# A rotary-embedding kernel on one core: a read of one row of `x` put first on ScalarE's DMA ring

## The chip, the cores and the metric

The kernel runs on one core of one Trainium2 chip. A time is the device time of one execution in microseconds (us). The core has five engines with instruction queues of their own: TensorE (PE) for matrix products, VectorE (DVE), ScalarE (ACT) and GpSimd (POOL) for elementwise work, and SyncE (SP), which here only issues DMA transfers. Transfers between the memory (HBM) and the core's SBUF are issued by SyncE and by ScalarE, each on a ring of its own, and are carried out by 16 DMA engines that both rings share.

## What is computed

Rotary position embedding with cached tables. `x` has the shape (8, 8, 1024, 64), the tables (1024, 32), all in float32:

```python
half = x.shape[-1] // 2
x_first, x_second = x[..., :half], x[..., half:]
out_first = x_first * cos_cached - x_second * sin_cached
out_second = x_first * sin_cached + x_second * cos_cached
return np.concatenate([out_first, out_second], axis=-1)
```

## The kernel before

`x` and the output are taken as 8 blocks (u = 0 to 7) of 128 partitions by 64 rows of 64 numbers; a block has 2 MB, and a partition holds 64 rows in sequence. All of `x` stays in SBUF, in the tiles `w0` to `w3`, which also have room for products (`sv`). The result is written over `x` in place and stored from there.

**Loads.** Line 76 has SyncE load the sine table, line 77 has ScalarE load the cosine table, each as 32 partitions by 1024 numbers (128 KB), into a part of `w0` that is free at that time (`rs`, `rc`). Then SyncE issues all loads of `x`: block 0 in two halves (line 81), blocks 1 to 7 whole (line 83). SyncE has nothing else to do but the stores (line 142), which come later in its queue.

**Tables.** A partition needs 64 rows of both tables, even partitions other ones than odd. GpSimd builds a unit matrix `plus` (lines 86, 87); ScalarE, whose first compute instruction brings a load of its function table with it, copies from it the selection matrix `sel` (line 89) and the negative `minus` (line 91). TensorE multiplies `sel` with the loaded tables and so spreads the first 32 rows of the sine table (`en`) and of the cosine table (`ec`) over 128 partitions (line 156), first `en`, then `ec`. For the other 32 rows VectorE shuffles the sine table and then the cosine table over 32 partitions (line 159), and ScalarE (line 160) and GpSimd (line 162) copy these to the other partitions. The shuffle of the cosine table and the product with it are the first readers of `rc`.

**Work.** Block 0 comes first: VectorE multiplies its first half with the tables straight from `en` and `ec` (line 106, called from 163 to 166), ScalarE copies its second half into PSUM (line 113, tile `pre`), VectorE multiplies that (line 172), and GpSimd adds up the products (lines 109, 110). Blocks 1 to 7 are cut into chunks of 24, 24 and 16 rows. For each, ScalarE copies the chunk into PSUM (`st`), VectorE makes both products in one instruction, and the sums are made either by GpSimd or, for 16 rows at a time, by TensorE (lines 184, 185) with ScalarE copying the result back (line 190). Half of block 2 is done by GpSimd alone. The order of all this is written out by hand in the lists `on_pe`, `back` and `behind`; a block is stored when its sums are done, the last block in three pieces.

The schedule is manual: each engine runs its instructions in the order in which the function issues them, and waits are set where an instruction reads or writes what another one wrote or read. The lines of the change stand between the definition of `rs` and `rc` and the two loads of the tables.

Of the kernel before, what the change touches and what calls it, by code (L numbers as in the profile page):

```python
# [8 lines left out]
def kernel(  # L9
# [7 lines left out]
    nc = tc.nc  # L17
    fp32 = mybir.dt.float32
# [3 lines left out]
    b, h, seq, hd = x.shape  # L22
# [12 lines left out]
    xf = x.rearrange("b h s d -> (b h s d)").rearrange(  # L35
        "(u p m) -> u p m", p=P, m=F)
# [4 lines left out]
    const = ctx.enter_context(tc.tile_pool(name="const", bufs=1))  # L41
# [31 lines left out]


    rs, rc = sv[3][0:Q, 0:C], sv[3][0:Q, C:2 * C]
    nc.sync.dma_start(out=rs, in_=sin_cached.rearrange("(q n) j -> q (n j)", q=Q))
    nc.scalar.dma_start(out=rc, in_=cos_cached.rearrange("(q n) j -> q (n j)", q=Q))

# [3 lines left out]
    for u in range(1, n_u):  # L82
# [7 lines left out]
                   in_=plus[0:Q, 0:Q:2].unsqueeze(1).to_broadcast([Q, 2 * P // Q, Q // 2]))  # L90
# [172 lines left out]
```

## Time and profile before

| | us |
|---|---|
| median of 7 runs | 85.33 |
| lowest, highest | 85.25, 85.5 |
| the profiled execution | 85.22 |
| its span, first to last instruction | 83.4 |

The profile is of one execution. A line of its group view gives the kernel's line, the engine, the operation, the tiles written and read, and how often, how long and after what idle time it ran; "q" behind an engine's name (SPq, ACTq) means its instruction queue, which issues DMAs. Busy time over the span: VectorE 82%, GpSimd 80%, TensorE 52%, ScalarE 49%.

| transfers, from the page | |
|---|---|
| moved | 33.82 MB in 2832 packets, 405 GB/s over the span |
| read, written | 17.04 MB, 16.78 MB |
| SyncE's queue | 2784 packets, 96.1% of 16 engines' span |
| ScalarE's queue | 48 packets, 0.4% |
| sine table, issue to landing | 3.0 us |
| cosine table, issue to landing | 3.4 us |

"Landing" is the time at which the transfer's semaphore tells that all of it has arrived. The DMA share of a stretch is the mean busy share of the 16 DMA engines in it.

### The profile page before, as it was taken

Reading aid. Unit: us, or ns where it says so; the run is one execution under the profiler, and the core shown is the slowest. Engines: PE = TensorE matmul, PEld = TensorE weight load, DVE = VectorE, ACT = ScalarE, POOL = GpSimd, SP = SyncE. Lnnn points to the kernel's source line nnn. Section 1 sums busy time; section 2 is a strip of 40 time slices with the busy share of each in tenths; the row PEclk is TensorE's granted clock in tenths of the full one; section 3 lists DMA queues with packets and bytes.
Section 4 is the critical chain, followed back from the end, with each engine's and each line's share of the span. In section 5 each row is a group of like instructions: output and inputs, shape, how many; then the busy total and the mean of one; then the engine's idle time right before and its main releaser. Section 6 shows DMA issues by size and latency. Waiting matters only on the chain.

```text
span 83.4 us, 386 instructions
## 1 busy us (share of the span) xinstructions
PE 43.7 (52%) x80; PEld 16.7 (20%) x80; DVE 68.5 (82%) x30; ACT 40.7 (49%) x36; POOL 67.1 (80%) x36
## 2 busy tenths in 40 slices
PE   0199920004991694949869494971964991000000
PEld 0133200002430332405133240411412330000000
DVE  0193999999999999999999999999999995890000
ACT  4409695364068548196176856675359208100000
POOL 3009809999999999999999999999999999991000
PEclk9999999999999999999999999999998579985555
DMA  2999999899998999999999999999999999999991
GB/s 31 295 428 448 432 424 456 377 487 393 424 456 377 487 393 440 440 401 479 377 393 456 409 448 432 432 432 416 456 401 440 440 432 440 416 440 383 424 416 65
DMA packets 2832, 33.82 MB, mean 405 GB/s; under 512 B 336, under 2 KB 336, under 8 KB 784
## 3 DMA queue, kind: packets, MB, share of 16 engines
q1 hardware_dynamic: 2784, 33.69, 96.1%
q10 hardware_dynamic: 48, 0.13, 0.4%
HBM read 17.04 MB, written 16.78 MB: 405 GB/s over the span
## 4 chain that ended last, share of the span: by engine, by line
POOL 64%; issue 13%; PE 5%; DMA 4%; DVE 3%; POOLq 2%
POOL w L110 26%; POOL w L109 24%; POOL w L106 14%; PE en L156 5%; DMA w<-in_sin_cached_dram 4%; DVE w L106 3%; POOLq L258 2%; POOLq L109 0%; POOLq L106 0%
## 5 line engine op out<-in xcount | busy, mean ns | idle before, releaser
L106 DVE TENSOR_TENSOR w<-st,tb 128x3072 f32<-128x3072 f32 (+2 forms) x19 | 54.7, 2952 | 1.2 <-ACT st L113 1.2
L113 ACT COPY st<-w 128x1536 f32<-128x1536 f32 (+1 forms) x19 | 24.9, 1310 | 15.7 <-DVE w L106 14.7
L184 PE MATMUL acc<-w,plus 128*128 128x512 f32 x36 | 21.1, 670 | 21.6 <-ACT w L190 12.6
L109 POOL TENSOR_TENSOR w<-w 128x1024 f32<-128x1024 f32 (+3 forms) x11 | 23.8, 2163 | 0.2
L110 POOL TENSOR_TENSOR w<-w 128x1024 f32<-128x1024 f32 (+3 forms) x11 | 23.8, 2164 | 0.0
L184 PEld LDWEIGHTS acc<-w,plus 128*128 128x128 f32 x36 | 6.7, 208 | 35.0 <-ACT w L190 19.2
L190 ACT COPY w<-acc 128x1024 f32<-128x1024 f32 x9 | 9.1, 1009 | 9.4 <-PE acc L185 9.4
L106 POOL TENSOR_TENSOR w<-w,tb 128x1280 f32<-128x1280 f32 x4 | 11.6, 2908 | 0.2
L185 PE MATMUL acc<-w,minus 128*128 128x512 f32 x18 | 10.8, 686 | 0.0
L185 PE MATMUL acc<-w,plus 128*128 128x512 f32 x18 | 9.2, 592 | 0.0
L162 POOL COPY tb<-tb 32x2048 f32<-32x2048 f32 x2 | 3.8, 1886 | 5.1 <-DVE tb L159 5.1
L156 PE MATMUL en<-w,sel 32*128 32x512 f32 x4 | 3.7, 1088 | 3.9 <-DMA w<-in_sin_cached_dram 3.9
L185 PEld LDWEIGHTS acc<-w,minus 128*128 128x128 f32 x18 | 4.0, 223 | 5.2 <-issue 5.2
L106 DVE TENSOR_TENSOR w<-pre,tb 128x4096 f32<-128x4096 f32 x1 | 4.4, 4415 | 0.0
L185 PEld LDWEIGHTS acc<-w,plus 128*128 128x128 f32 x18 | 3.4, 190 | 4.5 <-issue 4.5
L109 POOL TENSOR_TENSOR w<-w,w 128x1024 f32<-128x1024 f32 x1 | 2.3, 2326 | 2.2 <-issue 2.2
L156 PE MATMUL ec<-w,sel 32*128 32x512 f32 x4 | 3.6, 1056 | 0.0
L160 ACT COPY tb<-tb 32x2048 f32<-32x2048 f32 x1 | 1.9, 1897 | 3.3 <-DVE tb L159 3.3
L106 DVE TENSOR_TENSOR w<-w,en 128x2048 f32<-128x2048 f32 x1 | 2.3, 2287 | 1.4 <-PE en L156 1.4
L159 DVE LOAD_MASK_SELECT tb<-w x2 | 0.0, 8 | 3.8 <-DMA w<-in_sin_cached_dram 3.8
L159 DVE STREAM_SHUFFLE tb<-w 32x1024 f32<-32x1024 f32 x2 | 2.5, 1279 | 0.0
L106 DVE TENSOR_TENSOR w<-w,ec 128x1024 f32<-128x1024 f32 x2 | 2.4, 1217 | 0.0
(18 smaller groups left out, 14.2 us busy)
## 6 DMA issues: line engine op xcount, KB each, us to landing
w<-in_x_dram SPq DMA_DIRECT2D x7, 2048.0 KB, 24.8
out_dram<-w SPq DMA_DIRECT2D x7, 2048.0 KB, 10.5
w<-in_x_dram SPq DMA_DIRECT2D x2, 1024.0 KB, 6.3
out_dram<-w SPq DMA_DIRECT2D x2, 768.0 KB, 6.6
out_dram<-w SPq DMA_DIRECT2D x1, 512.0 KB, 6.6
w<-in_cos_cached_dram ACTq DMA_DIRECT2D x1, 128.0 KB, 3.4
w<-in_sin_cached_dram SPq DMA_DIRECT2D x1, 128.0 KB, 3.0
```

Source lines behind the costliest of these rows:

```text
L106: eng.tensor_tensor(out=o, in0=a, in1=t, op=TT.mult)
L109: eng.tensor_tensor(out=o[:, :, 0], in0=c[:, :, 0], in1=s[:, :, 1], op=TT.subtract)
L110: eng.tensor_tensor(out=o[:, :, 1], in0=c[:, :, 1], in1=s[:, :, 0], op=TT.add)
L113: nc.scalar.copy(out=pt[:, :(n1 - n0) * hd], in_=xt[u][:, n0 * hd:n1 * hd])
L156: nc.tensor.matmul(part, sel, r, start=True, stop=True)
L159: nc.vector.stream_shuffle(t[0:Q, H:], flat(r), odd)
L160: nc.scalar.copy(out=tb4[Q:2 * Q, H:], in_=tb4[0:Q, H:])
L162: nc.gpsimd.tensor_copy(out=tb4[k * Q:(k + 1) * Q, H:], in_=tb4[0:Q, H:])
L184: nc.tensor.matmul(a[:, k], plus, xr[:, :, k], start=True, stop=False)
L185: nc.tensor.matmul(a[:, k], plus if k else minus, sr[:, :, 1 - k], start=False, stop=True)
L190: nc.scalar.copy(out=rows(xt[u], n0, n0 + G), in_=a)
L258: with _tile.TileContext(nc) as tc:
```

## The change

A tile `row` of one partition by 64 numbers is added to the pool `const`, and ScalarE's first DMA becomes a read of the first row of block 0 of `x` into it. The cosine table is the second DMA on that ring. Nothing reads `row`; SyncE's transfers and all compute are as before.

```diff
     rs, rc = sv[3][0:Q, 0:C], sv[3][0:Q, C:2 * C]
+
+    row = const.tile([1, hd], fp32, name="row")
+    nc.scalar.dma_start(out=row, in_=xf[0][0:1, 0:hd])
     nc.sync.dma_start(out=rs, in_=sin_cached.rearrange("(q n) j -> q (n j)", q=Q))
     nc.scalar.dma_start(out=rc, in_=cos_cached.rearrange("(q n) j -> q (n j)", q=Q))
```

## The prediction

> **What bounds the kernel now.** I read the page's busy shares and its DMA line first, then a table of stretches with the DMA share of each, then the list of instructions in the first 14 us, then SyncE's waits.
>
> The DMA rows of the page, in 40 slices of 2.09 us:
>
> ```profile
> DMA  2999999899998999999999999999999999999991
> GB/s 31 295 428 448 432 424 456 377 487 393 424 456 377 487 393 440 440 401 479 377 393 456 409 448 432 432 432 416 456 401 440 440 432 440 416 440 383 424 416 65
> ```
>
> No compute engine fills its row like this: VectorE is busy 82% of the span and GpSimd 80%. The transfers work from the second slice to the last but one. The table of stretches (length, then each engine's busy time, TensorE's clock, DMA share, GB/s) makes it sharper:
>
> ```profile
> 1.50:2.00 0.50, 0.00 (x0) 0.00 (x0) 0.00 (x0) 0.50 (x1) 0.00 (x0) 1.00 1.04 115
> 2.00:2.50 0.50, 0.00 (x0) 0.00 (x0) 0.00 (x0) 0.49 (x2) 0.00 (x0) 1.00 0.37 106
> 2.50:3.00 0.50, 0.00 (x0) 0.00 (x0) 0.00 (x0) 0.48 (x2) 0.00 (x0) 1.00 1.37 426
> 3.00:4.00 1.00, 0.13 (x1) 0.16 (x1) 0.23 (x2) 0.00 (x0) 0.00 (x0) 1.00 0.93 291
> 4.00:20.00 16.00, 7.04 (x9) 2.37 (x9) 14.59 (x9) 8.77 (x8) 11.35 (x6) 1.00 1.03 435
> ...
> 70.00:80.00 10.00, 0.00 (x0) 0.00 (x0) 3.70 (x5) 1.15 (x2) 5.38 (x4) 0.72 0.98 417
> 80.00:81.00 1.00, 0.00 (x0) 0.00 (x0) 0.00 (x0) 0.00 (x0) 0.00 (x0) 0.50 1.02 418
> ```
>
> From 4 us to 81 us the engines' share is 1.0 (a packet is counted where it starts, hence 1.37 beside 0.37). So the end is the start of the stream, plus 33.8 MB at 417 to 435 GB/s, plus the last landing. The chain of waits on the page runs through GpSimd, but GpSimd ends at 75.4 us, and for 6 us after it only transfers work. A compute step that ends earlier gains nothing. One that ends later costs only where the stream would run dry.
>
> How near is that? SyncE issues stores 0 to 6 at 21.65, 35.27, 47.77, 52.39, 57.01, 63.78 and 70.31 us, and three pieces of the last block at 71.91, 75.41 and 75.84. When store 6 is issued, 17.04 MB of reads and six stores of 2.10 MB had been handed out, 29.62 MB; summing GB/s times length over all stretches up to 70.31 us gives 29.09 MB moved. The 0.53 MB left last 1.27 us at 417 GB/s. A new transfer needs about 1.02 us from its issue to its first packet (the sine table: issued at 0.74, first packet at 1.76 in the packet records). So compute may slip about **0.25 us** before the stream has a hole; store 6 has the least cover (store 5, by the same sum, has 3 us).
>
> The start, from the list of instructions (start, duration, instruction, what ended the idle time before):
>
> ```profile
> 0.73 0.41 ACTq L77 DMA_DIRECT2D w<-in_cos_cached_dram  x1
> ...
> 0.74 0.39 SPq L76 DMA_DIRECT2D w<-in_sin_cached_dram  x1
> ...
> 1.18 1.28 ACT L89 ACT_TABLE_LOAD   x1 [1.18 <-PEq L247]
> 1.18 0.89 SPq L81 DMA_DIRECT2D w<-in_x_dram  x2
> ...
> 3.87 3.75 PE L156 MATMUL en<-w,sel 32*128 32x512 f32 x4 [3.87 <-DMA w<-in_sin_cached_dram]
> ...
> 4.96 1.28 DVE L159 STREAM_SHUFFLE tb<-w 32x1024 f32<-32x1024 f32 x1
> ...
> 7.65 2.29 DVE L106 TENSOR_TENSOR w<-w,en 128x2048 f32<-128x2048 f32 x1 [1.41 <-PE en L156]
> ```
>
> The compute chain starts from the sine table: landed at 3.74 (3.0 after its issue), four matmuls, then VectorE at 7.65, after which VectorE hardly idles until 72 us. The cosine table lands at 0.73 + 3.4 = 4.13 and is first read at 4.96.
>
> **The change, part by part.** It adds one DMA of 256 bytes on ScalarE's ring, ahead of the cosine table, and 256 bytes of SBUF per partition. Nobody reads the row, so no compute instruction gets a wait on it. Nothing is removed. SyncE's program stands as it was, and nothing moves past POOL's queue.
>
> 1. *ScalarE's sequencer.* One more issue. DMA issues in this trace last 0.33 to 0.61 us, one lasts 1.22. I take the cosine table's 0.41. Everything behind it on ScalarE moves by 0.41: the table load from 1.18 to 1.59, the copy into `sel` (2.47 + 0.30) to an end at 3.18, `minus` (2.68 + 0.30) to 3.39. TensorE starts at 3.87, when the sine table is there: 0.48 us to spare even if it waits for both. At 1.22 us `minus` would end at 4.20, TensorE be 0.33 late, and with 0.25 us of cover the end moves by 0.08. Cost 0, upper end 0.08.
>
> 2. *The cosine table, 0.41 later.* At the same 3.4 us it lands at 4.54, still 0.42 ahead of the shuffle at 4.96. It now goes out at about the time of `x`'s first half, which takes 5.3 us from issue to landing; at that price it lands at 1.14 + 5.3 = 6.44. The shuffle would start 1.48 late, VectorE had 1.41 to spare ahead of 7.65, so it would be 0.07 late, inside the 0.25. ScalarE's copy of the table rows (6.27 to 8.17) would end at 9.65 and push the copy of `x` from 8.97 by 0.68, to an end at 11.52, before VectorE wants it at 12.20. GpSimd's copies (6.38 to 10.19) would end at 11.67, before 12.20 too. Cost 0 at both ends; the cover is VectorE's idle 1.41 us and the 0.83 before it, and without them each us would cost a us less 0.25.
>
> 3. *The row's own packets.* One data packet and its completion. ScalarE's queue now has 48 packets and 0.4% of 16 engines' span: 0.004 x 83.4 x 16 / 48 = 0.11 us each, for 4 KB pieces and completions. The row is less than one such piece. If its engine is the one that ends last, the end moves by 0.11 us at most; shared out over 16 it is 0.01. I take 0.02, for a packet this short is nearest to the completions.
>
> 4. *The sine table behind the row.* Both would come to the engines at about 1.76 us, on different rings. In the packet records each engine's first packet takes 0.43 to 0.72 us, its second 0.16 to 0.20. If the row is first on its engine, it either takes that opening time instead of the sine table (cost 0, nothing won, since 15 engines open as before) or adds its own (up to 0.72). The cosine table, issued in the same 10 ns as the sine table, had its first packets only after the sine table's second ones (2.51 us against 2.35), so ScalarE's ring has come second here. Cost 0, upper end in the second rival.
>
> 5. *Order of the completions.* The transfers' completions seem to be counted on eight semaphores in turn: SyncE's last load of `x` waits 1.4 us for an earlier one. With one more transfer in the count the fourth whole load (issued at 3.71) may have to wait for the row's landing, 3.74 to 4.13 by the tables' rows: up to 0.4 late. Ahead of it 8 MB are queued, over 15 us of work. Cost 0. After the last landing SyncE's waits follow at 0.06 us each, and one may change its place: 0.06 either way.
>
> Sum: 0 + 0 + 0.02 + 0 + 0. The profiled execution took 85.22 us, its span 83.4, with 1.8 around it; the median of the seven runs is 85.33, 0.11 higher. So 85.22 becomes 85.24, and the median 85.35.
>
> *Two rules weighed.* The trace has two small transfers issued 5 ns apart that landed 3.0 and 3.4 us later, so their waiting overlaps. The Trainium skill (DMA: Bandwidth & Descriptors, Anatomy of one DMA) gives every transfer a fixed cost of about 2 us and (Rules for kernel authors) says that transfers under 64 KB pay mostly overhead, which speaks against a 256-byte read. If these 2 us were served one after the other on the ring, the cosine table would land at 6.13 and the shuffle start 1.17 late, still inside VectorE's 1.41; by the row and by the rule the sum is the same. The same page (section on why a DMA increments its semaphore by 16) says that a transfer with no dimension to divide runs on one engine; no row here shows one. By that, point 3 touches one engine in 16.
>
> **Rivals.**
>
> *Faster: the row opens the stream.* At 3 to 4 us the share is 0.93 and the rate 291 GB/s, against 435 afterwards: `x`'s first packets take longer. If that is the price of first touching `x`, and the row pays it beside the sine table, (435 - 291) x 1 us = 0.144 MB, 0.33 us, comes off the stream, and with it off the end: 85.0. For it: packets right after are full speed. Against it: one row lies on one engine's path, and a slow start of any stream looks the same.
>
> *Slower: the row holds up the sine table.* One engine's share of the table comes after the row's own opening time, and the table counts as landed only with all its parts. It lands 0.43 to 0.72 late, at 4.17 to 4.46. TensorE, VectorE and all stores slip by that; less 0.25 the end moves by 0.18 to 0.47: 85.5 to 85.8. It decides from a landing later than 3.99. Against it: the order of the two rings, as in point 4.
>
> *Slower, less: a hole in the stream.* The cosine table's two packets of 0.16 us per engine now fill the time between the sine table and `x`. If they come later and `x` is not there yet, up to 0.32 us is idle: 85.4 to 85.65, middle 85.55.
>
> *It doesn't do what it says:* the unread row is dropped when the program is built. Then 85.33.
>
> **How the numbers follow.** Hidden as in the sum: 0.45, at 85.35. Dropped: 0.03. Opens the stream: 0.20, at 85.0. Holds up the sine table: 0.21, about 85.65. Hole: 0.11, about 85.55. A measurement of this kernel tells about 0.2%, 0.17 us, from no change. Faster by more 0.20, within 0.48, slower by more 0.32. The likeliest case alone spans 85.2 to 85.5; to leave out no more than 2 in 10 the range goes to 85.0 and 85.7.
>
> **What would show it.** Right: ScalarE's table load near 1.6, the sine table landing 3.0 after its issue, the shuffle at 4.96, VectorE's first product at 7.65, share 1.0 until 81 us, a third kind of DMA issue of 0.25 KB. Wrong: the sine table landing after 3.99, a share below 1 between 2.5 and 4 us or near 71 us, or a rate near 400 GB/s already at 3 us.

## The result and the profile after

| | before | after |
|---|---|---|
| median, us | 85.30 (37 runs) | 85.66 (14 runs) |
| lowest, highest | 85.09, 86.0 | 85.51, 85.83 |
| profiled execution, its span | 85.22, 83.4 | 85.76, 84.0 |

The ratio is 1.0041, 95% interval 1.0029 to 1.0053: slower by 0.25 to 0.45 us, about 0.36 in the medians and 0.54 between the two profiled executions.

The DMA rows of the page of the changed kernel (slices of 2.1 us):

```profile
DMA  1899999999999999998999999999999999999990
GB/s 25 246 373 414 441 476 398 437 429 429 445 382 476 398 437 429 429 445 382 484 390 453 421 429 437 421 445 406 468 390 468 406 445 421 429 437 388 424 419 33
```

Before, the first three slices moved 31, 295 and 428 GB/s; now 25, 246 and 373. Later the rates are alike, to the end. The table of stretches of the changed kernel (length, then each engine's busy time, TensorE's clock, DMA share, GB/s) shows the place:

```profile
1.50:2.00 0.50, 0.00 (x0) 0.00 (x0) 0.00 (x0) 0.37 (x1) 0.00 (x0) 1.00 0.39 74
2.00:2.50 0.50, 0.00 (x0) 0.00 (x0) 0.00 (x0) 0.50 (x1) 0.00 (x0) 1.00 1.50 369
2.50:3.00 0.50, 0.00 (x0) 0.00 (x0) 0.00 (x0) 0.49 (x2) 0.00 (x0) 1.00 0.44 82
3.00:3.50 0.50, 0.20 (x1) 0.23 (x2) 0.30 (x2) 0.43 (x2) 0.00 (x0) 1.00 0.44 82
3.50:4.00 0.50, 0.50 (x1) 0.27 (x2) 0.50 (x1) 0.00 (x0) 0.00 (x0) 1.00 0.84 328
4.00:20.00 16.00, 6.97 (x9) 2.49 (x8) 14.53 (x9) 9.21 (x8) 11.87 (x6) 1.00 1.03 429
```

The same table of the kernel before has for two of these stretches:

```profile
2.50:3.00 0.50, 0.00 (x0) 0.00 (x0) 0.00 (x0) 0.48 (x2) 0.00 (x0) 1.00 1.37 426
3.00:3.50 0.50, 0.00 (x0) 0.00 (x0) 0.00 (x0) 0.00 (x0) 0.00 (x0) 1.00 1.07 287
```

From 2.5 to 3.5 us it moved 426 and 287 GB/s; now both halves have 82. By 6 us the packet records have 1.09 MB landed instead of 1.32, and 0.23 MB are 0.53 us at 430 GB/s. The list of instructions of the changed kernel (start, duration, instruction, what ended the idle time):

```profile
0.73 0.50 ACTq L78 DMA_DIRECT2D row<-in_x_dram  x1
...
0.73 0.38 SPq L79 DMA_DIRECT2D w<-in_sin_cached_dram  x1
...
1.17 0.89 SPq L84 DMA_DIRECT2D w<-in_x_dram  x2
1.25 0.34 ACTq L80 DMA_DIRECT2D w<-in_cos_cached_dram  x1
1.63 1.28 ACT L92 ACT_TABLE_LOAD   x1 [1.63 <-PEq L250]
...
3.30 3.75 PE L159 MATMUL en<-w,sel 32*128 32x512 f32 x4 [3.30 <-ACT sel L92]
...
5.58 1.27 DVE L162 STREAM_SHUFFLE tb<-w 32x1024 f32<-32x1024 f32 x1
...
7.22 2.29 DVE L109 TENSOR_TENSOR w<-w,en 128x2048 f32<-128x2048 f32 x1 [0.36 <-DMA w<-in_x_dram]
```

And its DMA issues, with the time from issue to landing at the end of a line:

```profile
w<-in_sin_cached_dram SPq DMA_DIRECT2D x1, 128.0 KB, 2.4
w<-in_cos_cached_dram ACTq DMA_DIRECT2D x1, 128.0 KB, 4.3
```

Two things moved in opposite directions. The sine table lands 2.4 us after its issue instead of 3.0, and compute starts earlier: TensorE at 3.30 (before 3.87), VectorE's first product at 7.22 (7.65). The cosine table, issued 0.52 us later, needs 4.3 us instead of 3.4. Compute early, transfers late, time up: the transfers set the end.

Where is the hole? The first 16 packets of `x` start between 2.24 and 2.78 us, earlier than before (2.84 to 3.20). The next 16 start between 3.67 and 4.08 (before: 3.32 to 3.76), and in the gap the first packets of the cosine table come, from 3.32 on. So the engines do not stand idle ahead of `x`, but behind its first packets.

For the comparisons below I added up, from the packet records, the *loss*: how much longer the 16 engines took than their packets do undisturbed (159 ns for 4 KB, 309 for 8, 611 for 16), including the 1.75 us before the first. In the first 6 us this loss is 2.68 us before and 3.23 after, 0.55 more. At 40 to 44 us, where reading ends and storing begins, it is 0.19 before and 0.00 after; from 75 us on, where some engines end earlier than others, 0.16 and 0.30. The three add up to 0.50 us; the last packet ends 0.52 us later.

### The profile page after: what moved, and what is told of

It is laid out like the page before. It is cut to its first block, busy times and chain, and to the rows that moved or that the text cites. A ratio compares the mean times of both kernels' runs of the same rounds, so it can differ in the third digit from the quotient of the medians.

```text
span 84.0 us, 387 instructions
## 1 busy us (share of the span) xinstructions
PE 44.8 (53%) x80; PEld 17.0 (20%) x80; DVE 68.5 (82%) x30; ACT 40.7 (48%) x36; POOL 67.1 (80%) x36
## 4 chain that ended last, share of the span: by engine, by line
POOL 62%; issue 13%; DMA 7%; DVE 4%; POOLq 2%; SPq 0%; DVEq 0%
POOL w L112 24%; POOL w L113 24%; POOL w L109 14%; DMA w<-in_x_dram 7%; DVE w L109 4%; POOLq L261 2%; SPq L79 0%; POOLq L112 0%; DVEq L109 0%; POOLq L109 0%
## 5 line engine op out<-in xcount | busy, mean ns | idle before, releaser
L187 PE MATMUL acc<-w,plus 128*128 128x512 f32 x36 | 22.0, 696 | 19.8 <-ACT w L193 10.7
L187 PEld LDWEIGHTS acc<-w,plus 128*128 128x128 f32 x36 | 6.9, 211 | 33.3 <-ACT w L193 17.6
L188 PE MATMUL acc<-w,plus 128*128 128x512 f32 x18 | 9.7, 622 | 0.0
L188 PEld LDWEIGHTS acc<-w,plus 128*128 128x128 f32 x18 | 3.9, 219 | 5.4 <-issue 5.4
L112 POOL TENSOR_TENSOR w<-w,w 128x1024 f32<-128x1024 f32 x1 | 2.4, 2356 | 1.1 <-issue 1.1
L113 POOL TENSOR_TENSOR w<-w,w 128x1024 f32<-128x1024 f32 x1 | 2.4, 2377 | 0.0
```

The lines of the kernel that those rows point to most:

```text
L112: eng.tensor_tensor(out=o[:, :, 0], in0=c[:, :, 0], in1=s[:, :, 1], op=TT.subtract)
L113: eng.tensor_tensor(out=o[:, :, 1], in0=c[:, :, 1], in1=s[:, :, 0], op=TT.add)
L187: nc.tensor.matmul(a[:, k], plus, xr[:, :, k], start=True, stop=False)
L188: nc.tensor.matmul(a[:, k], plus if k else minus, sr[:, :, 1 - k], start=False, stop=True)
```

## The experiments

Two theories at first. *Late*: the row costs by putting off the cosine table's issue from 0.73 to 1.25 us, behind the first issue of `x` at 1.17, so that its packets reach the engines among those of `x` instead of ahead of them. *Touch*: the row's own read, of `x` or as one more transfer, does the harm. All ratios are to the kernel before, run on the same chip, with 95% intervals.

**The cosine table late, without a row** (e1)

```diff
+    nc.vector.memset(rc[:, 0:400], 0.0)
     nc.sync.dma_start(out=rs, ...)
     nc.scalar.dma_start(out=rc, ...)
```

> No row. ScalarE's issue of the cosine table waits for a VectorE memset of part of its destination, which should put it at about 1.2 us instead of 0.73, near the 1.25 of the changed kernel. Theory late (the row costs only because it moves the cosine table's issue by 0.52 us, so that its first packets fall among those of x and the engines stand idle): as slow as the change, +0.25 to +0.5 us over the kernel before, the sine table landing 2.4 to 2.5 us after its issue, idle engines between 2.5 and 3.5 us. Theory touch (the row's own read of x disturbs the first packets): as the kernel before, within 0.1 us. If the memset is short and the issue stays ahead of 1.0, the cost shrinks with it.

Measured: 85.60 against 85.34, ratio 1.0029 (1.0004 to 1.0054). From its list of instructions:

```profile
0.87 0.39 DVE L76 MEMSET w<- 32x400 f32 x1 [0.87 <-PEq L248]
...
1.30 0.37 ACTq L78 DMA_DIRECT2D w<-in_cos_cached_dram  x1
...
3.22 1.27 DVE L160 STREAM_SHUFFLE tb<-w 32x1024 f32<-32x1024 f32 x1
...
5.42 1.27 DVE L160 STREAM_SHUFFLE tb<-w 32x1024 f32<-32x1024 f32 x1
```

The table goes out at 1.30, and both signs of the change are there in compute without a row: the sine table early (the first shuffle at 3.22 instead of 3.77), the cosine table late (5.42 instead of 4.96). The time is that of *late*; the interval is wide and holds the whole cost of the change. The profiled execution (85.45, below this kernel's median) does not show the cost in the opening; the numbers are with the table further down.

**The row behind the cosine table** (e2)

```diff
     nc.sync.dma_start(out=rs, ...)
     nc.scalar.dma_start(out=rc, ...)
+    nc.scalar.dma_start(out=row, in_=xf[0][0:1, 0:hd])
```

> The same row, read second on ScalarE's ring, behind the cosine table, so that table goes out at 0.73 as before; the extra transfer, its semaphore and the 256 bytes of SBUF stay. Theory late: as the kernel before, within 0.1 us, with the sine table landing 3.0 us after its issue. Theory touch, if the touch or the extra transfer costs wherever it stands: +0.2 to +0.4 us.

Measured: 85.20, ratio 0.9985 (0.9971 to 1.0000). The same transfer, behind the cosine table instead of ahead of it, costs nothing; the sine table lands 2.9 us after its issue, as before. That ScalarE's table load now starts at 1.73 is hidden too.

**A row of the sine table ahead of the cosine table** (e5)

```diff
-    nc.scalar.dma_start(out=row, in_=xf[0][0:1, 0:hd])
+    nc.scalar.dma_start(out=row, in_=sin_cached[0:2, :].rearrange("(o n) j -> o (n j)", o=1))
```

> The change with another source: the 256 bytes read ahead of the cosine table come from the sine table, so x is not touched early. The kernel before gave 85.3, the change 85.66, the late cosine table without a row 85.6. Theory late (what counts is the issue of the cosine table at 1.25 us): as the change, 1.003 to 1.005 of the kernel before, engines half idle from 2.5 to 3.5 us. Theory touch (reading x early is what costs): as the kernel before, within 0.15 us.

Measured: 85.64 against 85.32, ratio 1.0033 (1.0017 to 1.0049), with the cosine table issued at 1.26. So it doesn't matter that the row is one of `x`. *Touch* has fallen three times: the cost comes without a row (e1), a row comes without the cost (e2), and another source costs the same (e5).

**A smaller delay** (e11): as e1, with `rc[:, 0:100]`.

> The late cosine table without a row, with a shorter memset, so that its issue comes at about 1.02 us, halfway between the kernel before (0.73) and the changed one (1.25). If the cost sets in where the cosine table's first packets no longer come ahead of x (x is issued at 1.17): as the kernel before or under half the change's cost, 1.000 to 1.002. If any delay costs in proportion: 1.002. If the order on the engines is lost already: 1.003 to 1.004.

Measured: 85.21 against 85.26, ratio 0.9992 (0.9979 to 1.0005). From its list of instructions:

```profile
0.98 0.37 ACTq L78 DMA_DIRECT2D w<-in_cos_cached_dram  x1
...
1.18 0.88 SPq L82 DMA_DIRECT2D w<-in_x_dram  x2
...
7.21 2.29 DVE L107 TENSOR_TENSOR w<-w,en 128x2048 f32<-128x2048 f32 x1 [1.41 <-PE en L157]
```

A delay of 0.25 us is free, one of 0.52 to 0.57 costs about 0.3 us. So it isn't delay in proportion, which would have given 1.002. The run also rules out that the earlier start of compute is what costs: VectorE's first product comes at 7.21 here, as early as in the changed kernel (7.22), and nothing is lost.

**Two rows** (e6): the change with a second row read behind the first.

> Two rows of x ahead of the cosine table, whose issue comes at about 1.7 us instead of 1.25. Theory late, if each 0.5 us of delay leaves the engines idle longer: 1.006 to 1.01. Theory late, if only the collision with the first packets of x counts: 1.002 to 1.005, no more than the change. Compute may add: the shuffle of the cosine table would start at about 6.1 us and VectorE's first product at about 7.4, no later than before.

Measured: 86.40, ratio 1.0121 (1.0104 to 1.0139). The second row's issue took 0.22 us, so the table went out at 1.52. VectorE's waits in the first 10 us:

```profile
DVE tb L163 <- DMA w<-in_cos_cached_dram: 3.5, 1, 3.5
DVE tb L163 <- DMA w<-in_sin_cached_dram: 3.3, 1, 3.3
```

The cosine table landed 6.5 us after its issue, at 8.05, and VectorE's first product began at 9.26. I had expected it at about 7.4, no later than before, and at most 1.01: a miss. VectorE is 1.61 us late, far beyond the cover of 0.25, yet nothing is lost near 71 us: the share is 1.01 from 66 to 74 us, and store 6 goes out at 70.11 (before: 70.31). The loss is 0.20 us more than before in the first 6 us, 0.60 between 6 and 8 us, where the cosine table's packets come to their end (5.24 to 6.93), and 0.61 more from 75 us on, where some engines end earlier than others. In order of the issue of the cosine table (the row kernels and e1, e11; packets from the packet records):

| | cosine table issued | its first packet | first packet of `x` | issue to landing | ratio |
|---|---|---|---|---|---|
| before | 0.73 | 2.51 | 2.84 | 3.4 | 1 |
| e2 | 0.73 | 2.41 | 2.73 | 3.3 | 0.9985 |
| e11 | 0.98 | 2.38 | 2.71 | 3.1 | 0.9992 |
| after | 1.25 | 3.32 | 2.24 | 4.3 | 1.0041 |
| e5 | 1.26 | 2.92 | 2.28 | 4.2 | 1.0033 |
| e1 | 1.30 | 3.49 | 2.25 | 4.0 | 1.0029 |
| e6 | 1.52 | 5.24 | 2.23 | 6.5 | 1.0121 |

The step lies between 0.98 and 1.25, where the order of the two issues turns (`x` at 1.17 to 1.18). Ahead of `x`, the cosine table's packets come before the first of `x`; behind it, they come 0.6 to 3 us after. That the order decides, and not some length of delay between 0.25 and 0.52 us, is likely but not shown: no run moved the issue of `x` alone.

Where the time goes is clear in after and e5, and not in e1. From the packet records of the profiled executions:

| | profiled, us | loss in the first 6 us | MB landed by 6 us | last packet ends |
|---|---|---|---|---|
| before | 85.22 | 2.68 | 1.32 | 82.02 |
| e2 | 85.33 | 2.79 | 1.27 | 82.11 |
| e11 | 85.26 | 2.84 | 1.27 | 81.99 |
| after | 85.76 | 3.23 | 1.09 | 82.54 |
| e5 | 85.65 | 3.09 | 1.16 | 82.43 |
| e1 | 85.45 | 2.82 | 1.29 | 82.18 |

After and e5 lose 0.25 us and more in the opening beyond e2 and e11, which are level with the kernel before in time; e1 does not. So the order of issue goes with the medians, but a larger loss in the opening is seen in after and e5 alone, and where e1 spends its 0.3 us stays open.

**The cosine table behind ScalarE's first copies** (e7): line 77 moved behind line 91, without a row.

> No row; the cosine table is issued by ScalarE behind its first two copies, at about 2.55 us, when x is under way. Theory late in its form that the harm is the opening (the cosine table's first packets come when the engines have had only one packet of x each and wait for the other ring): the stream is running when it comes, no idle stretch near 3 us for it, the sine table lands 2.4 us after its issue; within 0.15 us of the kernel before. Theory late in the form that every bit of delay costs: slower than the change, 1.006 and more. The shuffle would start at 6.3 to 6.6 us and VectorE's first product at 7.6 to 7.9, inside or just beyond the cover of 0.25 us.

Measured: 86.03, ratio 1.0107 (1.0087 to 1.0126), its seven runs spread from 85.49 to 86.38. The kernel wasn't what I meant it to be:

```profile
0.73 1.28 ACT L88 ACT_TABLE_LOAD   x1 [0.73 <-PEq L247]
...
1.34 0.37 ACTq L91 DMA_DIRECT2D w<-in_cos_cached_dram  x1
2.02 0.30 ACT L88 COPY sel<-plus 32x128 f32<-32x128 f32 x1
```

The transfer went out at 1.34, ahead of the copies written in front of it, so this is one more late cosine table (issue to landing 4.8 us, first packet at 3.67). Its issue is only 0.04 us behind that of e1, yet the median is 0.4 us higher; the profiled execution, 85.53, is among the fastest of its runs, and doesn't show where the rest goes. The run does not answer its question, and the higher median stays unexplained.

**Everything on SyncE's ring, without and with the row** (e3, e4): the cosine table issued by SyncE behind the sine table; in e4 the row alone on ScalarE's ring.

```diff
-    nc.scalar.dma_start(out=rc, in_=cos_cached...)
+    nc.sync.dma_start(out=rc, in_=cos_cached...)
```

> No row; the cosine table is issued by SyncE, between the sine table and x, so one ring carries everything and x is issued 0.45 us later. Theory late: the engines take the ring in order and no packet of x waits for another ring's turn; the sine table lands 2.4 us after its issue since nothing is read beside it, no idle stretch at 3 us. x starts when the tables are through. Time within 0.2 us of the kernel before, either way. A theory by which the delay of x's issue is what counts would have +0.4 us.

> As the one with both tables on SyncE's ring, and the row alone on ScalarE's. It isolates the row where it delays nothing. Theory late: equal to the kernel with both tables on SyncE's ring and no row, within 0.1 us. Theory touch: slower than that by 0.2 to 0.4 us, with the first packets of x longer. If the row opens x for the engines: faster by up to 0.3 us.

Measured: e3 86.00, ratio 1.0087 (1.0057 to 1.0117); e4 85.76, ratio 1.0047 (1.0030 to 1.0063). I had expected no difference for e3: a miss. Of the two theories named there, the one by which the later issue of `x` counts (now 1.63 us) had +0.4, nearer to both results; but the first packet of `x` starts at 2.80 in e3 and 2.79 in e4, no later than before (2.84). Both tables land early (2.5 and 2.6 us after their issues), and it is still slower. In the first 6 us its loss is 2.96 us, 0.28 more than before; at 40 to 44 us it is 0.46, 0.27 more. The row doesn't make e4 slower than e3, against *touch*; e4's cost in its profile is at the same two places (2.97 and 0.69).

**Without the cosine table, without and with the row** (e9, e10): the sine table is read in its place, so the output is another one.

```diff
-    rs, rc = sv[3][0:Q, 0:C], sv[3][0:Q, C:2 * C]
+    rs, rc = sv[3][0:Q, 0:C], sv[3][0:Q, 0:C]
...
-    nc.scalar.dma_start(out=rc, in_=cos_cached...)
```

> The cosine table is not loaded at all; the sine table is used in its place, so the output is another one, and 0.13 MB less is moved (0.31 us at 430 GB/s). Sine table and x alone open the stream. Theory turns (the late cosine table's packets on the other ring make engines wait while x is queued): without them the loss at the start is gone with the bytes, 0.3 us faster than the kernel before, 0.996 to 0.997. Theory cover (in the kernel before, the cosine table's packets fill the time until x's first packets arrive, and anything that takes them away leaves that time empty): the bytes saved are lost again as waiting, as the kernel before, 0.999 to 1.001.

> As the one without the cosine table (sine table in its place, another output), with the row alone on ScalarE's ring. The row delays nothing here. Theory late in both forms: equal to the one without row, within 0.1 us. Theory touch: 0.2 to 0.4 us slower.

Measured: e9 85.51 against 85.26, ratio 1.0020 (1.0002 to 1.0037); e10 85.53, ratio 1.0027 (1.0006 to 1.0047). The row by itself costs nothing that can be told. And a kernel that moves 0.13 MB less is no faster: *turns*, which had 0.3 us less, fails by the time, and *cover* (0.999 to 1.001) lies at the lower end of the interval. Two stretches of e9, one at the opening, one at 40 us:

```profile
2.50:3.00 0.50, 0.00 (x0) 0.00 (x0) 0.00 (x0) 0.03 (x1) 0.00 (x0) 1.00 0.16 33
...
40.00:42.00 2.00, 0.90 (x3) 0.30 (x2) 2.00 (x1) 1.37 (x2) 1.92 (x3) 1.00 1.06 287
```

In the opening the loss is 2.84 us against 2.68 before: of the 0.31 us that the bytes would save, half is waited away where the cosine table's packets used to be. That speaks for *cover*, but for half of the sum only. The rest of the time is at another place, the switch from reading to storing at 40 to 44 us, with a loss of 0.88 us (e10: 0.78; before: 0.19). So the total speaks against *turns* alone, and does not show that *cover* is the whole cause.

**Two other orders** (e8, e12): in e8 ScalarE issues the first half of block 0 behind the cosine table, in e12 it issues both tables and SyncE only `x`.

> No row, both tables as before; ScalarE issues the first half of block 0 of x behind the cosine table, SyncE the second half, so x is issued on two rings at 1.18 us. If the opening of the stream decides (the first packets of the rings cover each other, as the two tables do in the kernel before): 0.1 to 0.3 us faster than the kernel before, 0.997 to 0.999. If two rings side by side make the engines wait for one another: slower by 0.1 to 0.4 us.

> No row; ScalarE issues the sine and then the cosine table, SyncE starts at once with x, at 0.73 us. Theory turns: x's packets and the tables' come at the same time on two rings, the sine table lands late, 3.6 to 4.8 us after the start of its issue, and the stream has no gap between tables and x: the stream ends 0.2 to 0.4 us earlier if compute keeps up, but VectorE starts 0.5 to 1 us later than in the kernel before, beyond the cover of 0.25, and takes 0.3 to 0.7 us of it back: 0.998 to 1.005. If the opening of ScalarE's ring behind x is as slow as in the kernel with two rows: 1.01 and more.

Measured: e8 86.47, ratio 1.0117 (1.0092 to 1.0142); e12 86.35, ratio 1.0109 (1.0087 to 1.0131). e8 is slower than either case that I had named (at most 0.4 us); e12 fits its last case (1.01 and more). In e8 the first half of block 0 shares the engines with the second and lands 8.8 us after its issue; VectorE starts at 10.11, 2.46 late, and the stream gets the hole near 71 us that the cover of 0.25 us was about (before, the shares of these three stretches are 1.01, 1.00 and 0.95):

```profile
66.00:70.00 4.00, 3.00 (x7) 1.44 (x8) 4.00 (x2) 2.30 (x2) 4.00 (x3) 1.00 0.97 414
70.00:74.00 4.00, 0.70 (x2) 0.00 (x0) 3.65 (x3) 1.93 (x2) 4.00 (x3) 1.00 0.91 385
74.00:78.00 4.00, 0.00 (x0) 0.00 (x0) 2.43 (x3) 0.00 (x0) 3.73 (x3) 0.70 0.91 385
```

In e12 the tables are issued beside `x` from the start, and wait longest:

```profile
w<-in_sin_cached_dram ACTq DMA_DIRECT2D x1, 128.0 KB, 4.4
w<-in_cos_cached_dram ACTq DMA_DIRECT2D x1, 128.0 KB, 7.1
```

None of the versions is clearly faster than the kernel before; e2 and e11 are level with it.

## Why the prediction was right or wrong, point by point

The range held the time, by 0.04 us, and with some luck: of the weight at its upper end, more lay on the sine table held up (chance 0.21, about 85.65) than on the hole, and the table was not held up. The likeliest case, 85.35 and no difference, was the wrong one. The rival of a hole in the stream (chance 0.11, about 85.55) came nearest to the mechanism, though not to its place: it had the engines idle because `x` is not there yet, but `x` came earlier than before (2.24 instead of 2.84), and the idle time lies between its first packets and the next ones.

**What bounds the kernel**: right. The change started compute 0.43 us earlier and the time rose; e8 shows the other side, compute 2.46 us late, a hole at 70 to 78 us. The cover was taken too small, though. In e6 compute was 1.61 us late and the stream itself 0.80 by 8 us, in e8 2.46 and 0.26; with 0.25 us of cover they would have lost about 0.6 and 2.0 us near 71 us. They lost nothing and 0.7 there. Store 6 went out at 70.11 and 71.83 us (before: 70.31), so compute made up all or part of its delay; how is not shown.

**Point 1, ScalarE's sequencer**: right. One issue of 0.50 us for 0.41; table load at 1.63 for 1.59, `minus` at an end of 3.43 for 3.39. Since the sine table came earlier, TensorE now waits for `sel`; it still starts earlier than before.

**Point 2, the cosine table**: this step failed. It priced the delay by who reads the table, and there it held: the landing at 5.55 (4.54 taken, 6.44 as the bound), the shuffle at 5.58, VectorE's first product not late. It put at nothing, outside the rival, what the table's packets do for the stream: ahead of `x` they fill the engines' time, and behind the first issue of `x` they don't. e1 without a row and e11 with a smaller delay show that the late issue is what costs, and that it does so from somewhere between 0.98 and 1.25 us, where the order against `x` turns. The price, about 0.3 us in after, e1 and e5, is near the 0.32 us per engine of the rival (two packets of 0.16). That these packets' place in the opening explains all of it is not shown: e9 gives half, and in e1's profile the opening loses no more than in e11's.

**Point 3, the row's packets**: right. It is one data packet of 0.015 us and one completion of 0.009, so it ran on one engine in 16, as the prediction took it from the page; e10 against e9 and e2 against before show no cost.

**Point 4, the sine table**: cost 0 was right, "nothing won" was not. Its last packet ended at 2.46 us instead of 2.76, and the landing came 0.6 us sooner. e1 (2.50, without a row), e9 (2.45, without the cosine table) and e2 (2.72, with the row behind) point to the cause: the cosine table is no longer issued together with it. The gain ends in compute, which doesn't set the end. ScalarE's ring did not come second for the row: its packet was first of all, at 1.62 us.

**Point 5, the completions**: the cost of 0 was right, the wait was another: not the row's landing but that of the cosine table held up a load of `x`, for 0.6 us, and nothing followed from it that the profile shows.

**The rules weighed**: a fixed cost of the row did not show (e2). The section that the prediction cites for it (the Trainium skill, DMA: Bandwidth & Descriptors, Anatomy of one DMA) gives its 2 us for transfers issued from GpSimd, while these rings are SyncE's and ScalarE's; nothing in the sum rested on it. The same page, in Queues, rings and completion order, says that an engine takes turns, packet by packet, between the rings it has work for; if the late table was ready when `x` began, it would by that fall at most a few packets behind. With two rows (e6) its first packet came 3 us after that of `x`, when each engine had started seven packets of `x` on average. Whether the table's packets were ready earlier is not in the record.

**Rivals.** The row as an opener for `x`: against it, e5 is as slow with another source, and the first 16 packets of `x` took 0.73 us on average after, 0.54 before. The sine table held up: the opposite happened. Dropped: no, the issue is in the profile.

## What to carry to other kernels

When transfers set the end, price a moved transfer by its place in the stream as well as by its readers: here a small load that was issued before the big one rode in the time in which the big one's first packets were under way, and issued after it, it waited, and in the profiles of after and e5, not in that of e1, time was left empty there. Compare the issue times of all rings that share the engines, to a tenth of a microsecond; here 0.27 us lay between a delay that was free and one that cost. The unread transfer of 256 bytes cost nothing itself, and what stood behind it on its ring went out 0.5 us later.

## What the runs showed of the hardware that was not expected

- A small load issued together with another arrives later: the sine table's last packet ends at 2.72 to 2.76 us with the cosine table beside it (before, e2) and at 2.45 to 2.51 without (after, e1, e5, e6, e7, e9, e10). For the landing that is 2.9 to 3.0 us against 2.3 to 2.6.
- A table on ScalarE's ring issued 0.35 us after `x` began on SyncE's landed 6.5 us after its issue (e6); 0.2 us ahead of it, 3.1 (e11).
- A transfer written behind two copies on ScalarE went out ahead of them, at 1.34 us, while the copies ran from 2.02 to 2.53 (e7).
- The switch from reading to storing at 40 to 44 us cost 0.00 to 0.19 us in the kernels with the cosine table on ScalarE's ring, and 0.46 to 0.88 in the four without (e3, e4, e9, e10). The cause stays open; no run was made for it.
